# Two buffers in turn, in place of one allocated anew, for a norm's product of input and root

## The chip, the cores and the metric

One core of one Trainium2 chip runs the whole program in one launch. The metric is device time in microseconds (us) of that core, the median of the runs shown; lower is better. The names of the engines are those of the profile: PE is TensorE (PEld its weight loads), DVE is VectorE, ACT is ScalarE, POOL is GpSimd, SP is SyncE, which issues the DMAs.

## The reference, cut to what matters

Two layers of a block with four sequence mixers side by side, on 512 latent and 256 context tokens of width 1024. What the change touches is `modulate`, which stands ahead of the mixers and ahead of the feed-forward part in each layer.

```python
def rms_norm(x, g, eps=NORM_EPS):
    xf = x.astype(jnp.float32)
    y = xf * lax.rsqrt(jnp.mean(xf * xf, axis=-1, keepdims=True) + eps)
    return (y * g.astype(jnp.float32)).astype(x.dtype)

def modulate(x, g, shift, scale):
    return rms_norm(x, g) * (1 + scale) + shift
...
    for i in range(DEPTH):
        ...
        h_l = modulate(x, norm_mix_g[i], mod_l[0], mod_l[1])
        h_c = modulate(xc, norm_mix_g[i], mod_c[0], mod_c[1])
        pa_l, pb_l, pc_l, pd_l = _cumsplit(h_l @ w_in[i], MIXER_IN)
        ...
        x = x + mod_l[2] * (o_l @ w_out[i])
        x = x + mod_l[5] * conv_ffn(modulate(x, norm_ffn_g[i], mod_l[3], mod_l[4]),
                                    ffn_w_up[i], ffn_conv_w[i], ffn_conv_b[i], ffn_w_down[i])
```

## The kernel before

**Tiling.** The activations lie with their 1024 features on the partitions, as KD = 8 tiles `x[k]` of 128 features by up to 768 tokens. Each norm makes eight tiles `h[k]`, and each of these holds two halves, a high part `HL[:, 0]` and a low part `HL[:, 1]`, which the three matmuls of every product in `mm_feat` (L392) and the token-major products of `win_tok` (L770) read.

**The norm.** For each k, DVE multiplies `x[k]` by its scale and by the root into a scratch tile `y` (L641). ACT adds the shift and writes the high part (L643). For k = 0, 2, 3, 5 and 6 DVE makes the low part from `y` and the high part (L645). For k = 1, 4 and 7 (`k % 3 == 1`) ACT adds the shift into `y` in place (L648) and POOL makes the low part (L650). So `y` of k = 1, 4 and 7 is held until POOL is done with it.

There are seven such loops: the start norm of layer 0 (512 and 256 tokens one after the other under one `y` of 768 columns, the root `rs` in a tile of the on-chip memory SBUF), and then the feed-forward norm of layer 0, the mixer norm of layer 1 and the feed-forward norm of layer 1, each in two parts of tokens, a first loop and a second one (512 and 256 tokens, in the last norm 256 and 256). In these three the root lies in a bank of PSUM, the memory that PE writes (`pst`).

**Weights.** `weights` loads a piece by DMA, ACT writes its high part (L382, 512 or 288 columns) and POOL the low part (L383). POOL's queue is served in the order of the program, so these casts and the norm's L650 stand in one line. DVE's queue is in order too.

**Buffers.** `new` asks the `Arena` for columns: 30 slabs of 24 units (64 columns each), all columns of a slab of one type at a time. `find` takes, among the free places, the one that was given back longest ago, with a price for breaking into a slab that lies whole and idle. A place that is taken again waits for all earlier readers of it. In the start norm the arena has one place alone at that price, slab 9, so every `y` there is the same memory. In the feed-forward norm of layer 0 the eight `y` of the first loop lie in eight different places (in slabs 20, 13, 26, 20, 29, 24, 28 and 24). In the first loop of the mixer norm of layer 1 they alternate between slab 22 and slab 27 from k = 1 on. In the feed-forward norm of layer 1 they lie in eight places again.

**Order.** Program text is written by generators that are woven by a pace (`weave`); a scheduler then puts each engine's instructions in an order that follows which of them depend on which. The order is fixed when the program is built.

Of the kernel before, what the change touches and what calls it, by code (L numbers as in the profile page):

```python
# [223 lines left out]
class Net:  # L224
# [386 lines left out]
    def norm(self, li, which, x, sts, h, parts, first=None):  # L611

        nc = self.nc
        sh, sc = (0, 1) if which == "nmg" else (3, 4)
        gs = self.small([P, 8, 2], "gs")
        nco = self.conds(li, sc)

        def scales(k, m):
            nc.vector.scalar_tensor_tensor(out=gs[:, k:k + m, :nco], in0=self.mod[li][:, sc * 8 + k:sc * 8 + k + m, :nco], scalar=1.0,
                                           in1=self.par(li, which, k, m).unsqueeze(2).to_broadcast([P, m, nco]),  # L620
                                           op0=ALU.add, op1=ALU.mult)

        if first is None:
            scales(0, 8)
        n = parts[-1][-1][1]
        for i, (segs, st) in enumerate(zip(parts, sts)):
            a0, b0 = segs[0][0], segs[-1][1]
            w = b0 - a0
            if first is not None:
                rs = yield from self.root_first(first)  # L630
            else:
                rs = yield from self.root(st, segs)
            for k in range(KD):
                if first is not None:
                    scales(k, 1)
                if i == 0:
                    h.append(self.new([2, n], F32R))
                y, HL = self.new([w]), h[k]
                for a, b, s in segs:
                    yv, shift = y[:, a - a0:b - a0], self.modvec(li, sh, s, k)  # L640
                    nc.vector.scalar_tensor_tensor(out=yv, in0=x[k][:, a:b], scalar=gs[:, k, s:s + 1], in1=rs[:, a - a0:b - a0],  # L641
                                                   op0=ALU.mult, op1=ALU.mult)
                    nc.scalar.activation(out=HL[:, 0, a:b], in_=yv, func=AF.Identity, bias=shift)  # L643
                    if k % 3 != 1:
                        nc.vector.scalar_tensor_tensor(out=HL[:, 1, a:b], in0=yv, scalar=shift, in1=HL[:, 0, a:b].bitcast(F32),  # L645
                                                       op0=ALU.add, op1=ALU.subtract)
                    else:
                        nc.scalar.activation(out=yv, in_=yv, func=AF.Identity, bias=shift)  # L648
                if k % 3 == 1:
                    nc.gpsimd.tensor_tensor(out=HL[:, 1, a0:b0], in0=y, in1=HL[:, 0, a0:b0].bitcast(F32), op=ALU.subtract)  # L650
                self.free(y)
                if which == "nmg" and i + 1 == len(parts):
                    self.free(x[k])
                yield 1500 * w / T
            self.free(rs)


    def ffn(self, li, x, h, done, S):
# [1287 lines left out]
```

## Time and profile before

| | |
|---|---|
| median of 3 runs | 2377.65 us (2375.9 to 2383.59) |
| profiled execution, its own time | 2371.69 us |
| its span, first to last instruction | 2369.8 us |
| mean granted clock of PE in it | 0.954 |
| PE busy | 2194.0 us (93%) |
| DVE, POOL, ACT busy | 1327.0, 995.9, 934.2 us |

The profile is of one execution. Its own time stands 5.96 us below the median of the runs and 1.9 us above its span. Busy shares are means over stages; a busy PE need not be PE at its full rate, because the ends of matmuls are modelled.

### The profile page before, as it was taken

Reading aid. Unit: us, or ns where it says so; the run is one execution under the profiler, and the core shown is the slowest. Engines: PE = TensorE matmul, PEld = TensorE weight load, DVE = VectorE, ACT = ScalarE, POOL = GpSimd, SP = SyncE. Lnnn points to the kernel's source line nnn. Section 1 sums busy time; section 2 is a strip of 40 time slices with the busy share of each in tenths; the row PEclk is TensorE's granted clock in tenths of the full one; section 3 lists DMA queues with packets and bytes.
Section 4 is the critical chain, followed back from the end, with each engine's and each line's share of the span. In section 5 each row is a group of like instructions: output and inputs, shape, how many; then the busy total and the mean of one; then the engine's idle time right before and its main releaser. Section 6 shows DMA issues by size and latency. Waiting matters only on the chain. (4 is left out here: it accounts for less than half of the span.)

```text
span 2369.8 us, 40603 instructions
## 1 busy us (share of the span) xinstructions
PE 2194.0 (93%) x15656; PEld 1852.1 (78%) x15656; DVE 1327.0 (56%) x2900; ACT 934.2 (39%) x1730; POOL 995.9 (42%) x999
## 2 busy tenths in 40 slices
PE   7989996889989999999999989995899979999999
PEld 3877786768768788888888877785778868888888
DVE  3143567878864696765445643378877565332323
ACT  3333222555564422322223443332465544433333
POOL 1433437123422344434434634455443224555556
PEclk7999997889999999999999989997889989999999
DMA  8322354433234243343333521144233242333334
GB/s 324 116 72 82 102 150 108 105 89 93 58 123 143 82 137 116 109 142 106 116 107 107 172 65 55 59 126 132 69 98 87 77 138 72 102 94 99 98 98 134
DMA packets 241265, 258.51 MB, mean 109 GB/s; under 512 B 102896, under 2 KB 186160, under 8 KB 241072
## 3 DMA queue, kind: packets, MB, share of 16 engines
q1 hardware_dynamic: 241072, 255.92, 36.1%
q8 instruction: 123, 2.02, 0.4%
q14 instruction: 70, 0.57, 0.1%
HBM read 209.69 MB, written 37.77 MB: 104 GB/s over the span
## 5 line engine op out<-in xcount | busy, mean ns | idle before, releaser
L392 PE MATMUL pst<-slab,slab 128*128 128x512 f32 (+1 forms) x6552 | 1236.5, 350 | 14.4 <-POOL slab L650 5.8
L392 PEld LDWEIGHTS pst<-slab,slab 128*128 128x128 f32 x6552 | 1049.6, 190 | 195.8 <-issue 11.3
L383 POOL TENSOR_TENSOR slab<-slab,slab 128x512 fp32r<-128x512 f32 (+1 forms) x428 | 563.7, 1326 | 661.1 <-ACT slab L382 621.3
L382 ACT CAST slab<-slab 128x512 fp32r<-128x512 f32 (+1 forms) x428 | 258.7, 612 | 592.3 <-PE pst L392 418.6
L770 PE MATMUL pst<-slab,slab 128*128 128x256 f32 (+1 forms) x1872 | 254.1, 295 | 9.3 <-POOL slab L383 8.0
L770 PEld LDWEIGHTS pst<-slab,slab 128*128 128x128 f32 x1872 | 242.4, 199 | 20.4 <-POOL slab L383 9.5
L432 PE MATMUL pst<-cst,slab 128*128 128x128 f32 (+1 forms) x968 | 166.4, 305 | 69.1 <-DVE slab L937 21.7
L683 DVE SCALAR_TENSOR_TENSOR slab<-pst,pp,slab 128x511 f32<-128x511 f32 x66 | 41.6, 658 | 299.2 <-ACT slab L680 299.2
L432 PEld LDWEIGHTS pst<-cst,slab 128*128 128x128 f32 (+1 forms) x968 | 120.6, 153 | 96.6 <-DVE slab L937 24.3
L1620 PE MATMUL pst<-slab,slab 128*128 128x128 f32 (+4 forms) x1320 | 160.8, 283 | 7.3 <-DVE slab L1646 3.4
L1620 PEld LDWEIGHTS pst<-slab,slab 128*128 128x128 f32 (+3 forms) x1320 | 132.3, 179 | 29.6 <-issue 14.6
L714 DVE SCALAR_TENSOR_TENSOR slab<-pst,fgate,slab 128x512 f32<-128x512 f32 (+1 forms) x144 | 88.2, 628 | 104.9 <-PE pst L392 104.7
L1020 ACT ACTIVATE slab<-pst,mx 128x768 f32<-128x768 f32 (+1 forms) x120 | 97.7, 815 | 67.6 <-DVE mx L1018 64.3
L1018 DVE TENSOR_REDUCE mx<-pst 128x1 f32<-128x768 f32 (+1 forms) x120 | 100.2, 846 | 35.6 <-PE pst L1012 20.1
L695 POOL TENSOR_TENSOR slab<-slab,slab 128x768 fp32r<-128x768 f32 (+1 forms) x44 | 73.9, 1680 | 70.2 <-ACT slab L694 70.2
L551 DVE SCALAR_TENSOR_TENSOR slab<-slab,slab 128x512 bf16<-128x512 f32 x104 | 92.2, 886 | 5.1 <-DMA slab<-in_modw_dram 3.5
L1048 PE MATMUL pst<-slab,slab 128*64 128x128 f32 x832 | 67.0, 290 | 5.0 <-DVE slab L429 2.9
L1031 ACT ACTIVATE slab<-slab,r 128x768 f32<-128x768 f32 (+1 forms) x80 | 67.7, 852 | 10.0 <-DVE r L1030 9.3
L689 ACT ACTIVATE slab<-slab 128x768 f32<-128x768 f32 (+1 forms) x44 | 32.4, 737 | 85.7 <-DVE slab L685 85.6
L694 ACT CAST slab<-slab 128x768 fp32r<-128x768 f32 (+1 forms) x44 | 32.1, 729 | 85.0 <-DVE slab L691 84.9
L1012 PE MATMUL pst<-slab,slab 128*128 128x384 f32 (+1 forms) x144 | 48.8, 407 | 14.0 <-ACT slab L1020 6.4
L1048 PEld LDWEIGHTS pst<-slab,slab 128*64 128x64 f32 x832 | 46.9, 141 | 18.1 <-DVE slab L429 6.3
(320 smaller groups left out, 2626.6 us busy)
## 6 DMA issues: line engine op xcount, KB each, us to landing
slab<-in_wup_dram SPq DMA_DIRECT2D x88, 512.0 KB, 3.7
slab<-in_modw_dram SPq DMA_DIRECT2D x112, 256.0 KB, 3.0
slab<-in_wdn_dram SPq DMA_DIRECT2D x48, 512.0 KB, 3.5
slab<-in_win_dram SPq DMA_DIRECT2D x46, 512.0 KB, 3.9
slab<-in_modp_dram SPq DMA_DIRECT2D x40, 512.0 KB, 7.0
slab<-in_wout_dram SPq DMA_DIRECT2D x16, 512.0 KB, 3.7
slab<-in_xT_dram SPq DMA_DIRECT2D x16, 384.0 KB, 5.3
slab<-kb SPq DMA_DIRECT2D x24, 256.0 KB, 3.0
```

What stands on the lines that cost most here:

```text
L382: nc.scalar.copy(out=w[0], in_=st[:, k:k + q])
L383: nc.gpsimd.tensor_tensor(out=w[1], in0=st[:, k:k + q], in1=w[0].bitcast(F32), op=ALU.subtract)
L392: self.nc.tensor.matmul(ps[:, a:b], w[i][k][:, cols], x[j][k][:, a:b], start=(k == 0 and q == 0), stop=(k == nk - 1 and q == 2))
L432: self.nc.tensor.transpose(out, a.bitcast(F32) if a.dtype != F32 else a, self.c["ident"])
L551: self.tc.keep_in_program_order(nc.vector.scalar_tensor_tensor(out=junk, in0=w, scalar=1.0, in1=self.sc[s][e], op0=ALU.mult, op1=ALU.mult, ...
L695: nc.gpsimd.tensor_tensor(out=HL[:, 1, :n], in0=th[:, :n], in1=HL[:, 0, :n].bitcast(F32), op=ALU.subtract)
L714: nc.vector.scalar_tensor_tensor(out=x[m][:, a:b], in0=ps[:, a:b], scalar=gate[:, m, s:s + 1], in1=x[m][:, a:b], op0=ALU.mult, op1=ALU.add)
L770: self.nc.tensor.matmul(ps[:, :n], h[i][k][:, t * P:(t + 1) * P], w[j][k], start=(k == 0 and q == 0), stop=(k == KD - 1 and q == 2))
L1018: nc.vector.tensor_reduce(out=mx, in_=sv, axis=AX.XY, op=ALU.max, negate=True)
L1020: nc.scalar.activation(out=p[m][:, a:].rearrange("p (e c) -> p e c", e=2 - a // hb), in_=sv, func=AF.Exp, bias=mx, accum_out=lsum[:, m:m + 1])
L1048: nc.tensor.matmul(acc[64 * e:64 * e + 64, :P], vs[e][:, i + j], aT[:, 256 * j + P * e:256 * j + P * e + P], start=(first and j == 0), sto ...
L1620: mm = lambda o, a, b, pos: nc.tensor.matmul(o, a, b, start=True, stop=True, tile_position=pos)
```

## The change

The two buffers `ys` are taken before the loop over k, used in turn, and both are given back after the loop with the root.

```diff
@@ -630,12 +630,13 @@
                 rs = yield from self.root_first(first)
             else:
                 rs = yield from self.root(st, segs)
+            ys = [self.new([w]) for _ in range(2)]
             for k in range(KD):
                 if first is not None:
                     scales(k, 1)
                 if i == 0:
                     h.append(self.new([2, n], F32R))
-                y, HL = self.new([w]), h[k]
+                y, HL = ys[k % 2], h[k]
                 for a, b, s in segs:
                     yv, shift = y[:, a - a0:b - a0], self.modvec(li, sh, s, k)
...
                 if k % 3 == 1:
                     nc.gpsimd.tensor_tensor(out=HL[:, 1, a0:b0], in0=y, in1=HL[:, 0, a0:b0].bitcast(F32), op=ALU.subtract)
-                self.free(y)
                 if which == "nmg" and i + 1 == len(parts):
                     self.free(x[k])
                 yield 1500 * w / T
-            self.free(rs)
+            self.free(rs, *ys)
```

No instruction is added to the arithmetic or taken from it. What moves is memory: which place each `y` has, and with that the place of nearly every buffer that is taken later, and the order that the scheduler makes of it. The lines of `norm` behind the new one stand one line lower in the change: L641 is L642 there, L645 is L646, L650 is L651.

The first place is DVE's queue in the start norm, k = 1 to 3, before. The first name is what is written, and the digits behind slab9 count its tiles: slab9_13 is `y` (and the root, in other columns of the slab), slab4_8 to slab5_9 are `x`, slab12_27 and slab13_28 are `h[2]` and `h[3]`. In brackets stands the engine or DMA queue whose signal the instruction waits for.

```order
L641 SCALAR_TENSOR_TENSOR slab9_13_108<-slab4_8_103,gs_24_294,slab9_13_108 128x512 [waits DMAHW4_49,DVE_49]
L641 SCALAR_TENSOR_TENSOR slab9_13_108<-slab4_8_103,gs_24_294,slab9_13_108 128x256 [waits DVE_49]
L477 TENSOR_TENSOR mod0_77<-pst_69,pp_75 128x2x2 [waits PE_49,Activation_49]
L619 SCALAR_TENSOR_TENSOR gs_24_294<-mod0_77,pp_75 128x2 [waits DVE_49]
L641 SCALAR_TENSOR_TENSOR slab9_13_108<-slab5_9_104,gs_24_294,slab9_13_108 128x512 [waits DMAHW5_49,Pool_49]
L641 SCALAR_TENSOR_TENSOR slab9_13_108<-slab5_9_104,gs_24_294,slab9_13_108 128x256 [waits Activation_49]
L645 SCALAR_TENSOR_TENSOR slab12_27_336<-slab9_13_108,mod0_77,slab12_27_336 128x512 [waits Activation_49]
L645 SCALAR_TENSOR_TENSOR slab12_27_336<-slab9_13_108,mod0_77,slab12_27_336 128x256 [waits Activation_49]
L641 SCALAR_TENSOR_TENSOR slab9_13_108<-slab5_9_104,gs_24_294,slab9_13_108 128x512 [waits DMAHW6_49,DVE_49]
```

The same place in the change, from the second half of k = 1 to the first of k = 4:

```order
L642 SCALAR_TENSOR_TENSOR slab8_12_107<-slab4_8_103,gs_24_294,slab9_13_108 128x256
L477 TENSOR_TENSOR mod0_77<-pst_69,pp_75 128x2x2 [waits PE_49,Activation_49]
L642 SCALAR_TENSOR_TENSOR slab9_13_108<-slab5_9_104,gs_24_294,slab9_13_108 128x512 [waits DMAHW5_49,DVE_49]
L642 SCALAR_TENSOR_TENSOR slab9_13_108<-slab5_9_104,gs_24_294,slab9_13_108 128x256 [waits DVE_49]
L619 SCALAR_TENSOR_TENSOR gs_24_294<-mod0_77,pp_75 128x2
L619 SCALAR_TENSOR_TENSOR gs_24_294<-mod0_77,pp_75 128x2 [waits DVE_49]
L646 SCALAR_TENSOR_TENSOR slab12_27_336<-slab9_13_108,mod0_77,slab12_27_336 128x512 [waits Activation_49]
L646 SCALAR_TENSOR_TENSOR slab12_27_336<-slab9_13_108,mod0_77,slab12_27_336 128x256 [waits Activation_49]
L642 SCALAR_TENSOR_TENSOR slab8_12_107<-slab5_9_104,gs_24_294,slab9_13_108 128x512 [waits DMAHW6_49,Pool_49]
L642 SCALAR_TENSOR_TENSOR slab8_12_107<-slab5_9_104,gs_24_294,slab9_13_108 128x256
L642 SCALAR_TENSOR_TENSOR slab9_13_108<-slab6_10_105,gs_24_294,slab9_13_108 128x512 [waits DMAHW7_49,DVE_49]
```

The wait for POOL has moved from the product of k = 2 to that of k = 3, and two products and one low part stand between it and the one that POOL reads.

The second place is POOL's queue at the same time, from the low part of k = 1 on, before:

```order
L650 TENSOR_TENSOR slab11_26_327<-slab9_13_108,slab11_26_327 128x768 [waits Activation_49]
L650 TENSOR_TENSOR slab14_29_352<-slab9_13_108,slab14_29_352 128x768 [waits Activation_49]
L383 TENSOR_TENSOR slab3_4_99<-slab17_5_100,slab2_3_98 128x288 [waits DMAHW6_49,Activation_49]
L383 TENSOR_TENSOR slab3_4_99<-slab17_5_100,slab3_4_99 128x288 [waits Activation_49] x2
L383 TENSOR_TENSOR slab0_1_96<-slab18_6_101,slab0_1_96 128x288 [waits PE_49,DMAHW7_49,Activation_49,Pool_49]
L383 TENSOR_TENSOR slab0_1_96<-slab18_6_101,slab0_1_96 128x288 [waits PE_49,Activation_49,Pool_49]
L383 TENSOR_TENSOR slab1_2_97<-slab19_7_102,slab1_2_97 128x288 [waits DMAHW0_49,Activation_49,Pool_49]
L650 TENSOR_TENSOR slab8_32_377<-slab9_13_108,slab8_32_377 128x768 [waits Activation_49]
```

In the change the low part of k = 7 (slab28) stands behind one cast of the weights of `glav`, not six:

```order
L651 TENSOR_TENSOR slab11_26_327<-slab8_12_107,slab11_26_327 128x768 [waits Activation_49]
L651 TENSOR_TENSOR slab14_29_352<-slab9_13_108,slab14_29_352 128x768 [waits Activation_49]
L383 TENSOR_TENSOR slab3_4_99<-slab17_5_100,slab2_3_98 128x288 [waits DMAHW6_49,Activation_49]
L651 TENSOR_TENSOR slab28_32_377<-slab8_12_107,slab28_32_377 128x768 [waits Activation_49]
L383 TENSOR_TENSOR slab3_4_99<-slab17_5_100,slab3_4_99 128x288 [waits Activation_49] x2
```

The third place is DVE's queue in the feed-forward norm of layer 0, in the change. There slab27 holds both `y` of the first loop (512 columns), slab25 and slab10 the two of the second (256 columns); slab15, slab25 and slab4 are `x` as the second name.

```order
L642 SCALAR_TENSOR_TENSOR slab27_23_171<-slab15_108_3829,gs_327_7141,pst_69 128x512 [waits PE_49]
L642 SCALAR_TENSOR_TENSOR slab27_23_171<-slab15_108_3829,gs_327_7141,pst_69 128x512
L642 SCALAR_TENSOR_TENSOR slab25_21_169<-slab15_108_3829,gs_327_7141,pst_69 128x256 [waits PE_49]
L646 SCALAR_TENSOR_TENSOR slab16_213_5541<-slab27_23_171,mod0_77,slab16_213_5541 128x512 [waits Activation_49]
L642 SCALAR_TENSOR_TENSOR slab10_88_3483<-slab15_108_3829,gs_327_7141,pst_69 128x256
L642 SCALAR_TENSOR_TENSOR slab27_23_171<-slab25_21_169,gs_327_7141,pst_69 128x512 [waits DVE_49]
L646 SCALAR_TENSOR_TENSOR slab16_213_5541<-slab25_21_169,mod0_77,slab16_213_5541 128x256 [waits Activation_49]
L642 SCALAR_TENSOR_TENSOR slab27_23_171<-slab4_8_103,gs_327_7141,pst_69 128x512 [waits Pool_49]
```

Before, the first loop's products came one after the other with no wait for POOL, and the second loop's behind them; in the change the two loops are interleaved, and the product of k = 3 waits for POOL.

## Rows read from the trace of the kernel before

**Rows 1.** The page: PE's busy time, PE's busy tenths and its granted clock.

```profile
PE 2194.0 (93%) x15656; PEld 1852.1 (78%) x15656; DVE 1327.0 (56%) x2900; ACT 934.2 (39%) x1730; POOL 995.9 (42%) x999
...
PE   7989996889989999999999989995899979999999
...
PEclk7999997889999999999999989997889989999999
```

**Rows 2.** Busy time by stretch: from:to, length, engines with counts, clock, DMA.

```profile
41.50:76.40 34.90, 30.87 (x181) 21.79 (x177) 17.25 (x31) 17.36 (x37) 14.21 (x12) 0.96 0.46 157
...
830.00:1370.00 540.00, 536.76 (x3051) 466.96 (x3049) 328.50 (x604) 157.54 (x238) 237.20 (x159) 1.00 0.40 124
...
1600.00:1800.00 200.00, 157.69 (x1278) 135.46 (x1278) 163.53 (x414) 94.09 (x194) 85.79 (x145) 0.85 0.36 98
...
1641.80:1646.50 4.70, 4.27 (x19) 3.87 (x20) 4.26 (x19) 3.00 (x7) 0.00 (x0) 0.50 0.41 67
```

**Rows 3.** Waits of PE over the whole span: total us, times, longest.

```profile
PE pst L432 <- DVE slab L937: 21.7, 10, 7.1
...
PE pst L1465 <- DVE slab L1443: 10.1, 1, 10.1
```

**Rows 4.** DVE in order of time in the start norm: start, us, what.

```profile
48.39 1.15 DVE L641 SCALAR_TENSOR_TENSOR slab<-slab,gs,slab 128x512 f32<-128x512 f32 x2 [2.64 <-POOL slab L650]
49.93 1.15 DVE L645 SCALAR_TENSOR_TENSOR slab<-slab,mod,slab 128x512 fp32r<-128x512 f32 x2 [0.40 <-ACT slab L643]
...
58.12 0.16 DVE L477 TENSOR_TENSOR mod<-pst,pp 128x4 f32<-128x4 f32 x1 [3.12 <-PE pst L474]
58.43 2.23 DVE L641 SCALAR_TENSOR_TENSOR slab<-slab,gs,slab 128x512 f32<-128x512 f32 x2
60.58 2.23 DVE L645 SCALAR_TENSOR_TENSOR slab<-slab,mod,slab 128x512 fp32r<-128x512 f32 x2
```

**Rows 5.** POOL in order of time in the same stretch.

```profile
46.55 1.80 POOL L650 TENSOR_TENSOR slab<-slab,slab 128x768 fp32r<-128x768 f32 x1 [13.73 <-ACT slab L648]
...
58.36 2.96 POOL L383 TENSOR_TENSOR slab<-slab,slab 128x288 fp32r<-128x288 f32 x3
...
68.94 1.81 POOL L650 TENSOR_TENSOR slab<-slab,slab 128x768 fp32r<-128x768 f32 x1 [4.26 <-ACT slab L648]
71.98 0.80 POOL L383 TENSOR_TENSOR slab<-slab,slab 128x288 fp32r<-128x288 f32 x1 [1.23 <-ACT slab L382]
73.74 2.03 POOL L383 TENSOR_TENSOR slab<-slab,slab 128x288 fp32r<-128x288 f32 x2 [0.96 <-ACT slab L382]
```

**Rows 6.** ACT in order of time in the same stretch.

```profile
44.34 1.12 ACT L643 ACTIVATE slab<-slab,mod 128x512 fp32r<-128x512 f32 x2
45.36 1.11 ACT L648 ACTIVATE slab<-slab,mod 128x512 f32<-128x512 f32 x2
```

**Rows 7.** PE by line and shape, 41.5 to 76.4 us: count, busy us, mean ns, idle.

```profile
L392 PE MATMUL pst<-slab,slab 128*128 128x512 f32 x48 | 18.2, 437 | 3.4 <-POOL slab L650 2.6 <-ACT slab L643 0.8
...
L770 PE MATMUL pst<-slab,slab 128*128 128x288 f32 x29 | 5.6, 306 | 0.2 <-POOL slab L383 0.2
L470 PE MATMUL pst<-slab,slab 128*32 128x256 f32 x44 | 4.7, 457 | 0.0
L474 PE MATMUL pst<-cst,slab 128*128 128x2 f32 x12 | 1.6, 239 | 0.2 <-ACT slab L472 0.2
```

**Rows 8.** The same view of PE, 830 to 1370 us.

```profile
L392 PE MATMUL pst<-slab,slab 128*128 128x512 f32 x1515 | 517.2, 398 | 0.0
```

**Rows 9.** PE in order of time behind the start norm.

```profile
76.44 18.39 PE L770 MATMUL pst<-slab,slab 128*128 128x288 f32 x139
```

**Rows 10.** Waits of DVE, 1375 to 1400 us (mixer norm of layer 1).

```profile
DVE slab L641 <- POOL slab L650: 2.9, 2, 2.0
```

**Rows 11.** Waits of PE on POOL, 800 to 820 us, then 1375 to 1400 us.

```profile
PE pst L392 <- POOL slab L650: 0.8, 2, 0.6
...
PE pst L392 <- POOL slab L650: 1.9, 3, 1.1
```

## The prediction

> **What bounds the kernel now.** I began with the page. PE is busy for 2194.0 of 2369.8 us [rows 1], so most of the span is PE's work, and the change takes none of it away. What it can win or lose is time in which PE waits or runs slowly. The slices show where: the first ones, two groups in the middle of either layer (the mixers), and nothing in the feed-forward stages. The table by stretch says the same in microseconds: from 830 to 1370 us, the feed-forward of layer 0, PE lacks 3.2 of 540 us, from 1600 to 1800 us, the mixers of layer 1, 42.3 of 200 us at a mean granted clock of 0.85 [rows 2]. Then the list of PE's waits: in the mixers they are a handful of single long ones, such as 10.1 us on one DVE product at L1443 and 21.7 us in ten waits on L937 [rows 3]. Last I read the norms in order of time, engine by engine, since the change sits there.
>
> In the start norm the single `y` is a chain. DVE's product of k = 2 stands idle for 2.64 us until POOL's low part of k = 1 (46.55 us, 1.80 us long) has let go of `y` [rows 4, 5]. DVE's next long idle time, 3.12 us ahead of L477, ends in the product of k = 5 at 58.43 us [rows 4]. That product has to wait for POOL's low part of k = 4 in any case; L477, which waits for PE, only hides it. From 58.36 us on POOL casts weights, and DVE's pairs of halves take 2.23 us in place of 1.15 [rows 4, 5]. The last low part on POOL ends at 70.75, the last cast at 75.77, and at 76.44 PE begins a closed run of 139 products [rows 5, 9].
>
> **Does PE have room there?** From 41.5 to 76.4 us it runs 48 pairs of products of 512 and 256 columns, 29 of 288, 44 of L470 and 12 of L474 [rows 7]. A pair costs 536.76 / 1515 = 0.354 us where PE is saturated [rows 2, 8], a product of 288 columns 18.39 / 139 = 0.132 us [rows 9]. So 48 x 0.354 = 17.0, 29 x 0.132 = 3.8, and L470 and L474 at most the 4.7 and 1.6 us that they show: 27.1 of 34.9 us [rows 2]. At most 7.8 us can be won here, however fast DVE gets.
>
> **The change part by part.** *Start norm.* With two buffers the product of k = 2 no longer stands behind POOL. DVE is free at 48.39 - 2.64 = 45.75, so the product ends at 46.9. ACT is done with L648 at 46.47 [rows 6], writes the high part of k = 2 by 48.0, its first half by 47.6. The low part on DVE then meets POOL's L650, which runs to 48.35.
>
> Can the two run together? Beside POOL's casts the two halves of a product took 2.23 us in place of 1.15, so DVE lost 1.08 us, while POOL did 2.23 / 2.96 x 3 x 0.80 = 1.8 us of its own work [rows 4, 5]: DVE stood for some 60% of POOL's time. For a single long L650 I let it wait to the end, the worse case. The Trainium skill (SBUF — State Buffer, "Who interferes with whom") says that a DVE instruction with two inputs in SBUF and a GpSimd instruction that reads SBUF hold each other off, and whichever comes second waits for the whole instruction. By that rule the start comes out as below; by the 60% of the trace alone it would win 0.7 us more at each of two places.
>
> So the low part of k = 2 starts at 48.4 in place of 49.93, 1.5 us earlier. From there DVE has low part, product, low part, product with nothing to wait for (in the new order L477 stands behind the whole norm): 4 x 1.15 = 4.6, and the product of k = 5 starts at 53.0, not 58.43. The low part of k = 5 must let L650 of k = 4 pass (its `y` is ready 1.15 for the product, 0.5 for the last high half and 0.5 for the shift later, so at 54.0, and it ends at 55.8); then low part, product, low part, product of k = 5 to 7 take 4 x 1.15 = 4.6 us, to 60.5. Two more halves on ACT and the cast that stands between bring L650 of k = 7 to 61.8, where it started at 68.94 [rows 5]: 7.1 us earlier. It is faster than the waits alone because five casts now stand behind it, not ahead. They must be paid: seven casts of 0.80 us behind 63.6 end at 69.2, not 75.77, 6.6 us earlier. PE's closed run should begin 6 us earlier. I take **-6.0**. The low end is -1.5 (only the first wait goes, the rest is lost to casts and port), the high end -7.8. A loss of any weight I exclude here: every `y` is free no later than before, and at worst seven casts of 0.80 behind 70.75 would end at 76.35, 0.6 us late. PE is full behind 76.44, so what is won is not idle time that was there anyway.
>
> *Feed-forward norm of layer 0.* Here eight places become two a loop, and the change adds waits for POOL where there were none; behind the waiting product stand the low parts on which PE's products wait. The price is in the trace: the mixer norm of layer 1 alternated between two places already and lost 2.9 us of DVE to L650 [rows 10], and PE lost 1.9 us to POOL there against 0.8 in this norm [rows 11]. The difference at PE is 1.1. The new order interleaves the two loops and covers part of it. I take **+1.0**, ends 0 and +2.9.
>
> *Mixer norm of layer 1.* It has two places before and after; the second loop now comes in between and fills waits: **-0.5**, ends -2.9 (all of the wait goes) and +1.0. *Feed-forward norm of layer 1.* As in layer 0, with loops of half the length: **+0.5**, ends 0 and +1.5.
>
> *Everything else.* Nearly every later buffer has another place, so other reuses set other waits. In the feed-forward stages PE lacks 3 us in 540 [rows 2], nothing to win, and the other engines have slack to hide a wait. In the mixers it can go either way. One wait of the size of the longest single one is 10.1 us [rows 3]; I take **0** and the ends -10 and +12.5 (below).
>
> **Sum.** -6.0 + 1.0 - 0.5 + 0.5 = -5.0. The profiled execution took 2371.69 us and would take 2366.7. The median of the runs is 5.96 us above it, so the changed kernel's median should be 2377.65 - 5.0 = 2372.65, say **2372.7 us**. About 0.3% (7.1 us) is what a measurement of this kernel can tell from no change: under 2370.5 is faster, above 2384.8 slower.
>
> **Rivals.** *The start's gain is small.* If DVE and POOL block each other through the casts too, or PE's queue, which is in order, holds a product that waits for a late cast ahead of ready ones, only the first wait's 1.5 us is left, and the norms of the feed-forward take 1.5 back: 2377.7. For it: the casts are moved into a row behind L650, and POOL works them off alone. Against it: PE has 7.8 us of room and the last `h` comes 7 us earlier.
>
> *One long wait more in the mixers (slower).* At L1465 PE stood 10.1 us for DVE's product at L1443, and once only [rows 3]. DVE is busy there for 163.5 of 200 us [rows 2], so an operation that a reused place lets in late, or one that the new order puts ahead, makes PE wait in a second place. A wait of that size also lowers the granted clock: behind a wait of 7.1 us on L937 the profile shows 0.50 for another 4.7 us with 4.27 us of busy PE [rows 2, 3]; that work would take half as long at the upper level, so the wait costs about 2.4 us more. 10.1 + 2.4 = 12.5 on top of -5.0 gives 2385.2, slower. It decides from 12.1 us on (5.0 + 7.1); a second wait of only 7 us would leave no change. Against it: the order in the mixers follows the same dependences.
>
> *One long wait less in the mixers.* By the same reasoning the 10.1 us may go, by 8 to 10 us: 2363 to 2365. Nothing in the profile favours the one sign over the other.
>
> *The change does nothing.* Outside the start `y` mostly had several places already; were the start hidden, the time would be 2377 to 2379. PE's closed run from 76.44 speaks against it. I count it with the small gain.
>
> **How the numbers follow.** The start keeps its gain and the rest is even: 0.42, 2368 to 2378. Small or hidden gain: 0.17, 2375 to 2381. Longer waits in the mixers: 0.22, from 2383 up. Shorter ones: 0.19, below 2370. Of the first case I put 0.17 below 2370.5, since 2372.7 is only 2.2 us from that bound, and of the third 0.02 stays within. Faster: 0.19 + 0.17 = 0.36. Slower: 0.20. Same: 0.44. The range goes from 2361 to 2387: the low end is the sum with the longest mixer wait gone and 1.6 us more of the start, the high end the slower rival and 2 us. Beyond either end I leave about one chance in ten. The likeliest case's own range is 2368 to 2378.
>
> **What would show it.** In the changed profile the wait of L642 for L651 ahead of the product of k = 2 should be gone; the last L651 of the start should begin near 62, the last cast of `glav` near 69, PE's closed run of L770 near 70. In the feed-forward norm of layer 0 DVE should show one to three us of waits for L651, and PE's waits on it should go from 0.8 to about 1.9. The feed-forward stages should keep their length within 1 us. The prediction is wrong if PE's closed run starts later than 74, or if the stretches from there to the first feed-forward norm, or from 1420 to 1980, change by more than 5 us.

## The result, and the profile after

The changed kernel takes 2402.56 us (median of 4 runs, 2401.3 to 2404.56) against 2376.78 us of the kernel before beside it (4 runs, 2374.79 to 2383.59): a ratio of 1.0117, 95% interval 1.0094 to 1.014 (the quotient of the two medians is 1.0108, inside that interval). It is slower by 26 us. The profiled execution took 2404.56 us with a span of 2402.7 us, 32.9 us more than that of before. It is the slowest of its four runs, and the profiled execution of before was a fast one, so some 7 of the 32.9 us are the scatter of single executions. In the lines from 634 to 651 the numbers stand one higher than before (L641 is L642, L650 is L651).

The page of the change first, PE's busy time, its busy tenths and its granted clock, as in [rows 1]:

```profile
PE 2212.3 (92%) x15656; PEld 1860.7 (77%) x15656; DVE 1340.4 (56%) x2900; ACT 936.1 (39%) x1730; POOL 1004.9 (42%) x999
...
PE   7989996799989899999999989985799989999999
...
PEclk8999997889899999999999999997789999999999
```

Same 15656 products, 18.3 us more of PE's busy time, and the thin slices are again those in the mixers. To place the loss I matched the traces: the n-th product of each line and shape before with the n-th after; the edge of a stage moves by the median shift of the products within 8 us of it. By that the start is 4.8 us faster (0.4 was lost on entry already), the mixers of layer 0 take 14.4 us more, the feed-forward norm of layer 0 2.4 more, the mixer norm of layer 1 1.6 less, the mixers of layer 1 19.0 more and the last norm 3.5 more. With 0.3 us less between norm and mixers of layer 1 this makes 0.4 - 4.8 + 14.4 + 2.4 - 1.6 - 0.3 + 19.0 + 3.5 = 33.0, the 32.9 of the span. The feed-forward stages keep their length within 0.1 us.

The start is what was asked for. In the change, DVE and then POOL in order of time, to be held against [rows 4, 5]:

```profile
45.67 0.16 DVE L477 TENSOR_TENSOR mod<-pst,pp 128x4 f32<-128x4 f32 x1 [2.42 <-PE pst L474]
45.78 2.71 DVE L642 SCALAR_TENSOR_TENSOR slab<-slab,gs,slab 128x512 f32<-128x512 f32 x2
48.56 1.14 DVE L646 SCALAR_TENSOR_TENSOR slab<-slab,mod,slab 128x512 fp32r<-128x512 f32 x2
...
54.60 2.21 DVE L646 SCALAR_TENSOR_TENSOR slab<-slab,mod,slab 128x512 fp32r<-128x512 f32 x2 [0.29 <-ACT slab L644]
```

```profile
45.93 2.28 POOL L651 TENSOR_TENSOR slab<-slab,slab 128x768 fp32r<-128x768 f32 x1 [13.09 <-ACT slab L649]
54.04 1.83 POOL L651 TENSOR_TENSOR slab<-slab,slab 128x768 fp32r<-128x768 f32 x1 [5.83 <-ACT slab L649]
...
61.38 1.84 POOL L651 TENSOR_TENSOR slab<-slab,slab 128x768 fp32r<-128x768 f32 x1 [0.73 <-ACT slab L649]
63.18 5.39 POOL L383 TENSOR_TENSOR slab<-slab,slab 128x288 fp32r<-128x288 f32 x7
```

No product waits for POOL's L651 any more; the last L651 starts at 61.38, not 68.94, and seven casts end at 68.57. PE behind it:

```profile
66.58 3.34 PE L770 MATMUL pst<-slab,slab 128*128 128x288 f32 x24
69.84 1.07 PE L470 MATMUL pst<-slab,slab 128*32 128x256 f32 x16
70.84 0.79 PE L770 MATMUL pst<-slab,slab 128*128 128x288 f32 x4
71.47 0.54 PE L474 MATMUL pst<-cst,slab 128*128 128x2 f32 x4
71.87 18.39 PE L770 MATMUL pst<-slab,slab 128*128 128x288 f32 x139
```

The closed run begins at 71.87, not 76.44 [rows 9], and PE no longer waits for the casts: what stands ahead follows without a gap. So the loss lies in the two mixer stages, none of whose statements the change touches. Their windows, first of before, then of the change (length, then busy time with counts, last clock, DMA share, GB/s):

```profile
78.00:784.00 706.00, 639.26 (x5463) 535.89 (x5462) 421.51 (x1028) 296.87 (x599) 252.14 (x319) 0.93 0.36 102
...
1556.00:1982.00 426.00, 363.91 (x3287) 311.48 (x3286) 300.55 (x722) 203.86 (x413) 166.94 (x235) 0.92 0.39 105
```

```profile
73.60:794.00 720.40, 648.34 (x5462) 541.73 (x5461) 419.87 (x1030) 296.95 (x600) 258.55 (x319) 0.92 0.35 100
...
1566.40:2011.40 445.00, 374.47 (x3287) 315.13 (x3286) 311.58 (x720) 204.61 (x413) 167.67 (x235) 0.91 0.37 101
```

Length less PE's busy time is PE's idle time: 66.7 and 72.1 us in layer 0, 62.1 and 70.5 in layer 1. So of the 14.4 us 5.3 are idle, of the 19.0 us 8.4; the rest, 9.1 and 10.6 us, is the same products taking longer. Part of that is the clock: by the trace's clock record PE was at the lower of its two levels for 119.5 us of the mixers of layer 0 (95.6 before) and for 78.5 us of those of layer 1 (71.7 before). Half of each difference, 12 and 3.4 us, is an estimate of the most that this costs. It covers the longer products of layer 0 and only a third of those of layer 1.

### The profile page after: what moved, and what is told of

The parts are those of the page before. It is cut to its first block, busy times and chain, and to the rows that moved or that the text cites. A ratio compares the mean times of both kernels' runs of the same rounds, so it can differ in the third digit from the quotient of the medians.

```text
span 2402.7 us, 40609 instructions
## 1 busy us (share of the span) xinstructions
PE 2212.3 (92%) x15656; PEld 1860.7 (77%) x15656; DVE 1340.4 (56%) x2900; ACT 936.1 (39%) x1730; POOL 1004.9 (42%) x999
## 5 line engine op out<-in xcount | busy, mean ns | idle before, releaser
L770 PE MATMUL pst<-slab,slab 128*128 128x256 f32 (+1 forms) x1872 | 256.1, 297 | 29.2 <-POOL slab L383 13.3
L770 PEld LDWEIGHTS pst<-slab,slab 128*128 128x128 f32 x1872 | 244.6, 200 | 39.4 <-POOL slab L383 14.0
L432 PE MATMUL pst<-cst,slab 128*128 128x128 f32 (+1 forms) x968 | 171.1, 305 | 60.9 <-DVE slab L937 24.0
L432 PEld LDWEIGHTS pst<-cst,slab 128*128 128x128 f32 (+1 forms) x968 | 119.6, 152 | 91.3 <-DVE slab L937 24.3
L1620 PE MATMUL pst<-slab,slab 128*128 128x128 f32 (+5 forms) x1304 | 157.9, 280 | 9.4 <-DVE slab L1646 3.2
L1020 ACT ACTIVATE slab<-pst,mx 128x768 f32<-128x768 f32 (+1 forms) x120 | 97.7, 816 | 73.3 <-DVE mx L1018 72.2
L551 DVE SCALAR_TENSOR_TENSOR slab<-slab,slab 128x512 bf16<-128x512 f32 x132 | 113.8, 862 | 4.9 <-DMA slab<-in_modw_dram 2.9
L695 POOL TENSOR_TENSOR slab<-slab,slab 128x768 fp32r<-128x768 f32 (+1 forms) x44 | 74.1, 1685 | 72.2 <-ACT slab L694 72.2
L1048 PE MATMUL pst<-slab,slab 128*64 128x128 f32 x808 | 69.2, 299 | 7.1 <-DVE slab L429 5.2
L1707 POOL TENSOR_TENSOR slab<-cst,pcu 64x256 f32<-64x256 f32 x48 | 30.9, 644 | 83.1 <-PE pst L1620 41.1
```

The source lines that it names most:

```text
L432: self.nc.tensor.transpose(out, a.bitcast(F32) if a.dtype != F32 else a, self.c["ident"])
L551: self.tc.keep_in_program_order(nc.vector.scalar_tensor_tensor(out=junk, in0=w, scalar=1.0, in1=self.sc[s][e], op0=ALU.mult, op1=ALU.mult, ...
L695: nc.gpsimd.tensor_tensor(out=HL[:, 1, :n], in0=th[:, :n], in1=HL[:, 0, :n].bitcast(F32), op=ALU.subtract)
L770: self.nc.tensor.matmul(ps[:, :n], h[i][k][:, t * P:(t + 1) * P], w[j][k], start=(k == 0 and q == 0), stop=(k == KD - 1 and q == 2))
L1020: nc.scalar.activation(out=p[m][:, a:].rearrange("p (e c) -> p e c", e=2 - a // hb), in_=sv, func=AF.Exp, bias=mx, accum_out=lsum[:, m:m + 1])
L1048: nc.tensor.matmul(acc[64 * e:64 * e + 64, :P], vs[e][:, i + j], aT[:, 256 * j + P * e:256 * j + P * e + P], start=(first and j == 0), sto ...
```

## The experiments

Two theories. **Places**: the second buffer does in the norms what it should; what costs is that both are held through the loop, so that nearly every later buffer gets another place, with it other waits and another order of each queue. **Two buffers**: the alternation itself lets engines run ahead and makes something later stand. The first four kernels take the change apart.

*a_two_old_places.* The start norm alone, with the allocator's books as before:

```diff
+            if first is not None:
+                odd = self.slabs.tile([P, Arena.SLAB * Arena.GRAN], F32, tag="slab29", name="odd", bufs=1)[:, :w]
...
+                own = y
+                if first is not None and k % 2:
+                    y = odd
...
-                self.free(y)
+                self.free(own)
```

> The kernel before, but the start norm's product alternates between its own slab and one that lies unused until the mixers; the allocator's books and every place handed out later are those of before, and so is each engine's order from the start's end on. Later norms keep what they had. Theory 'places' (the two buffers gain in the start, the loss comes from where all later buffers land and from the order that follows): the closed run of token-major matmuls starts 4 to 5 us earlier than in the kernel before, mixers of both layers keep their lengths within 2 us, total 2371 to 2374 (4 to 6 below before). Rival 'two buffers' (the alternation itself makes something later stand): the mixers grow as in the change, total 2390 or more.

2370.66 us, ratio 0.9989 (0.9978 to 1.0). The start gains 4.5 us, the mixers are 707.0 and 426.6 us long, 1.0 and 0.6 more than in before. By time it lies 2.1 us below the kernel before beside it, where 4 to 6 were expected.

*d_one_new_places.* The places of the change, one buffer used:

```diff
-                y, HL = ys[k % 2], h[k]
+                y, HL = ys[0], h[k]
```

> The change with one index: every norm holds its two buffers as in the change, but uses the first of them for all eight products, so the places of all buffers are those of the change and the use of one buffer is that of before. Theory 'places': the mixers of layer 0 still take some 18 us more than in before, those of layer 1 some 19 more; the start's gain of 4.5 is gone and the later norms lose a little from one buffer alone: 2404 to 2415. Rival 'two buffers': with one buffer in use the loss of 25 is gone, 2376 to 2385.

2412.55 us, ratio 1.0161 (1.0139 to 1.0184). The start's gain is gone, the mixers of layer 1 lose 23.6 us. This falls to "places". Its mixers of layer 0, however, lose only 2.6 us where 18 were expected: their idle time is that of the change (72.2 us), their busy time is not (636.4 against 648.3). The last section comes back to it.

*s_start_only* and *l_later_only.* The change in the first norm or in the later three alone, the other norms as before:

```diff
+            two = first is not None
+            ys = [self.new([w]) for _ in range(2)] if two else []
...
+                y, HL = ys[k % 2] if two else self.new([w]), h[k]
...
+                if not two:
+                    self.free(y)
```

(`first is None` in the other.)

> The change in the first norm alone; the three later norms take and free one buffer a product as in before. Up to the first FFN norm each engine's order and every place is that of the change, afterwards the places are a new draw, neither those of before nor of the change. Theory 'places': start 4.5 less and mixers of layer 0 some 18 more, exactly as in the change (first FFN norm about 10 later than before); mixers of layer 1 are a new draw, anywhere from 10 less to 20 more than in before: total 2377 to 2407. Rival 'two buffers in the later norms' is what costs: mixers of layer 0 would be as in before and the total 2372.

2391.1 us, ratio 1.0072 (1.0053 to 1.0092). Mixers of layer 0 11.4 us longer, of layer 1 14.9. The expectation's 18 for layer 0 had counted from the best point behind the start; from edge to edge the change had 14.4.

> The change in the three later norms alone; the first norm as before. Up to the first FFN norm each engine's order and every place is that of before, afterwards the places are a new draw. Theory 'places': start and mixers of layer 0 equal before within 1 us; the two FFN norms with two halves of one slab cost 2 to 4 us each as in the change, since before's places for the product were already several; mixers of layer 1 a new draw, from 10 less to 20 more: total 2372 to 2403. Rival 'two buffers in the first norm make the mixers of layer 0 late' is not excluded by this run, but one that puts the loss on the later norms' two buffers expects 2400 or more here.

2387.68 us, ratio 1.0059 (1.0039 to 1.0079). Start and mixers of layer 0 as before (706.1 us), the two feed-forward norms 3.5 us longer each, the mixers of layer 1 8.6 longer: a new draw in the range named.

*after_again.* The change a second time, for its profile.

> The change once more, unedited, for a second profile of it. In the first profile the mixers of layer 0 lost 14.5 us against before, some 5 of them as idle time of TensorE and 9 as a lower granted clock; the kernel with one buffer in use, whose queues there stand in the same order and whose waits are the same, lost 2.6. If the clock's part is luck of one execution, this profile shows the mixers of layer 0 within 5 us of before; if it repeats with the order and its timing, 11 to 15 again, and the lower clock at the same gaps near 618 to 636. Mixers of layer 1: 19 again by either. Time 2401 to 2405.

2400.06 us, one execution. Layer 0's mixers lose 9.5 us this time, layer 1's 18.3. The first value lies under the 11 to 15 of a repeat and over the 5 of luck: about half repeats.

*u_hold, u_turn4, u_away28.* No norm is changed. Each edit gives later buffers other places:

```diff
         self.weave(start())
+        hold = self.new([256])
```

```diff
-    LOW, TURN, BREAK, AWAY = 17, 5, 100, 30
+    LOW, TURN, BREAK, AWAY = 17, 4, 100, 30
```

(and 28 for AWAY in the third).

> The kernel before, with no norm changed: after the first norm it reserves 256 columns of buffer that nothing ever writes or reads, so that the allocator hands out other places for what follows. Same instructions, same work. Theory 'places': start and first norm equal before within 1 us, the mixers of either layer a new draw, each from 5 less to 20 more; total 2372 to 2410, and a difference of more than 3 us from before in at least one mixer stage. Rival 'the loss belongs to the norms' two buffers': within 3 us of before in each stage, total within 0.3%.

> The kernel before with no norm changed and one number of the allocator's pricing moved from 5 to 4, which moves later buffers to other places from the middle of layer 0's mixers on. Theory 'places': everything up to some 300 us equal before; then each mixer stage a new draw, from 5 less to 20 more; total 2372 to 2410. Rival 'two buffers': within 0.3% of before.

> The kernel before with no norm changed and another number of the allocator's pricing moved from 30 to 28, a third draw of places for all that follows the first 250 us or so. Theory 'places': each mixer stage a new draw, from 5 less to 20 more; total 2372 to 2410. Rival 'two buffers': within 0.3% of before. If this and the other two redraws all come out slower than before, the places of before are a good draw rather than a middling one, and a change that redraws them pays for that on average.

2395.42 us, ratio 1.0083 (1.0054 to 1.0112); 2382.71, 1.0051 (1.003 to 1.0072); 2386.5, 1.0047 (1.0019 to 1.0074). All slower, by the mixers of layer 1: 18.2, 10.0 and 11.0 us more. A buffer that nothing touches costs two thirds of what the change costs.

*f_load_place.* One wait of the changed order by itself. In the change SP's queue in layer 1's mixers, in order of time:

```profile
1618.37 1.57 SPq L1509 DMA_DIRECT2D slab<-scrin  x2
...
1628.86 1.25 SPq L1509 DMA_DIRECT2D slab<-scrin  x2
1630.15 0.61 SPq L1626 DMA_DIRECT2D slab<-vt  x1
1630.81 1.06 SPq L376 DMA_DIRECT2D slab<-in_win_dram  x2
```

The list of SP's waits from 1605 to 1650 us says what the second L1509 waited for (total us, times, longest):

```profile
SPq L1509 <- DVE slab L1438: 8.1, 1, 8.1
```

A load of the recurrent scan stands ahead of two weight loads and waits for its place. PE, in order of time, then stands twice for those weights:

```profile
1635.29 0.80 PE L770 MATMUL pst<-slab,slab 128*128 128x256 f32 x2 [8.12 <-ACT slab L382]
1645.06 1.22 PE L770 MATMUL pst<-slab,slab 128*128 128x256 f32 x4 [8.97 <-POOL slab L383]
```

The edit was meant to put that one buffer into a slab that is idle:

```diff
             nd, ao = BD[d][i % 2], self.new([4, 64])
+            if (li, d, i) == (1, 0, 0):
+                at = self.shaped(self.slab[24][:, 0:256], [4, 64])
+                self.held[id(at)] = (at,) + self.held.pop(id(ao))[1:]
+                ao = at
```

> The change with one 256-column buffer of layer 1's recurrent scan (the first chunk's block of scores, loaded at L1509) put into a slab that is idle instead of the place that the allocator gives it, and nothing else: all other places stay, and the engines' queues keep their order but for 4 entries on SP, 4 on POOL, 2 on ACT, 5 on VectorE and some 26 matmuls. In the change that load stands on SP's queue ahead of two weight loads and waits 8.1 us for VectorE; the weights then come late and TensorE stands 8.1 us for their cast and 9.0 us for their split. Theory 'places act through the order of the queues': without that wait the weight load leaves some 10 us earlier (near 1621 in place of 1630.8), the two waits of TensorE shrink from 17 together to under 11, and layer 1's mixers give back 4 to 10 us: 2392 to 2399. Rival 'the weights' split was late anyway', since POOL is held by the features' chain until 1643: the load leaves earlier, TensorE stands as long for POOL, and the total stays at 2400 to 2405.

2395.91 us, ratio 1.0104 (1.0084 to 1.0124), within the change's interval. The first weight load leaves at 1613.33 in this run, where the stage is 8.4 us ahead of the change's, so 9 us earlier. The second stays behind the scan's load, which still waits for DVE, and longer than in the change. The list of SP's waits from 1600 to 1645 us (the load's L1509 is L1513 in this kernel):

```profile
SPq L1513 <- DVE slab L1442: 10.6, 1, 10.6
```

So slab 24 was not idle: in this program L1442 of DVE still reads the columns that the load is to overwrite. The edit did not take the wait away, it let one of the two weight loads out from behind it. PE:

```profile
1620.95 0.38 PE L770 MATMUL pst<-slab,slab 128*128 128x256 f32 x1 [2.14 <-ACT slab L382]
1631.29 3.13 PE L770 MATMUL pst<-slab,slab 128*128 128x256 f32 x13 [9.96 <-POOL slab L383]
...
1638.68 3.83 PE L770 MATMUL pst<-slab,slab 128*128 128x256 f32 x15 [4.04 <-POOL slab L383]
```

17.1 us of waits have become 16.1: the cast comes 6 us sooner to PE, and PE stands for POOL, whose next piece of that weight is queued behind L1446, which waits for DVE. The mixers of layer 1 take 447.8 us, nothing is given back there; where this profile is shorter than that of the change it is in layer 0's mixers (710.6 us), which the edit does not reach. The total lies in the range of the theory and below that of the rival, but not by the stage that the theory named. What is shown is this much: with the first weights on their way 9 us earlier PE's products with POOL's part of them begin 5.4 us earlier in the stage (1631.29 in place of 1645.06), then PE stands 4.0 us for POOL's part of the second weights, and nothing of it is left. That speaks for the rival, POOL being held by other work. What the scan's wait costs stays open, because no run here is without it.

*c_all_two_old.* The counterpart to d: the change's two buffers in all four norms, with every other place and, outside the norms, every queue's order as before. To the edit of a comes

```diff
+            else:
+                q, s0 = {(0, "nfg", 0): (24, 0), (0, "nfg", 1): (24, 16), (1, "nmg", 0): (26, 0), (1, "nmg", 1): (26, 0),
+                         (1, "nfg", 0): (23, 0), (1, "nfg", 1): (23, 0)}[li, which, i]
+                two = [self.slab[q][:, s0 * 64 + e * w:s0 * 64 + e * w + w] for e in range(2)]
...
+                if first is None:
+                    y = two[k % 2]
+                elif k % 2:
+                    y = odd
```

> The change's two buffers in turn in all four norms, with the place of every other buffer and every queue's order outside the norms as in the kernel before: the allocator keeps the books of before, and each later norm's products alternate between two halves of a slab that is idle during it. Theory 'places': start 4 to 4.5 less; the two FFN norms 2 to 4 us longer each, since before gave their eight products eight places and two in turn are fewer; mixer norm of layer 1 from 2 less to 1 more; layer 0's mixers 705 to 710 and layer 1's 424 to 428 as in before (706 and 426), not 716 to 721 and 444 to 448 as in the change. Total within 5 us of before, ratio 0.998 to 1.002. Rival 'two buffers': the mixers lengthen as in the change, 2390 or more.

2372.98 us, ratio 1.0002 (0.9986 to 1.0018). Its windows from the start's end to the last norm:

```profile
73.70:780.40 706.70, 639.26 (x5462) 535.74 (x5462) 422.19 (x1034) 297.69 (x601) 253.09 (x319) 0.93 0.35 104
780.40:821.30 40.90, 34.81 (x199) 29.37 (x198) 28.12 (x73) 20.38 (x37) 16.41 (x14) 0.83 0.24 78
...
1556.30:1983.30 427.00, 364.66 (x3287) 311.92 (x3286) 300.60 (x722) 203.61 (x413) 167.49 (x235) 0.91 0.38 105
1983.30:2034.80 51.50, 46.79 (x292) 40.70 (x291) 28.93 (x70) 25.40 (x49) 24.73 (x22) 0.97 0.21 66
```

Two buffers without the new places cost nothing and win nothing: the mixers are those of before to 1 us, the feed-forward norms are longer by 2.9 and 3.5 us, and that eats the start.

*a_again.* The one version that might beat the kernel before, in five rounds.

> The version with the second buffer in the start norm alone and all other places as before, timed in five rounds to see whether it beats the kernel before by more than the measurement can miss. From the first profile of it (start 4.1 less, layer 0's mixers 1.0 more, layer 1's 0.6 more): 2.5 to 4.5 less, ratio 0.998 to 0.9995. Rival 'two buffers cost elsewhere': ratio 1.000 or more.

2371.17 us, ratio 0.9998 (0.9986 to 1.001). The start gains 4.0 us in its profile once more, but by time it is not told from before. No version here beats the kernel before by more than can be measured.

All stages side by side, in us, from one profile each; "start" is the shift behind the start norm less that at 20 us, in brackets PE's idle time, the length less PE's busy time:

| kernel | start | mixers 0 | ff norm 0 | mixers 1 | ff norm 1 |
|---|---|---|---|---|---|
| before | 0 | 706.0 (66.7) | 38.0 | 426.0 (62.1) | 48.0 |
| the change | -4.8 | 720.4 (72.1) | 40.4 | 445.0 (70.5) | 51.5 |
| after_again | -4.8 | 715.5 (73.3) | 40.2 | 444.3 (68.5) | 52.0 |
| f_load_place | -4.1 | 710.6 (72.3) | 40.3 | 447.8 (66.3) | 51.9 |
| d_one_new_places | -0.3 | 708.6 (72.2) | 40.0 | 449.6 (69.9) | 52.1 |
| s_start_only | -4.4 | 717.4 (71.6) | 38.6 | 440.9 (71.6) | 48.4 |
| l_later_only | -0.3 | 706.1 (67.6) | 41.5 | 434.6 (68.4) | 51.5 |
| u_hold | -0.3 | 704.7 (76.2) | 39.3 | 444.2 (75.7) | 47.9 |
| u_turn4 | -0.3 | 705.2 (71.1) | 37.7 | 436.0 (70.1) | 48.0 |
| u_away28 | -0.1 | 703.4 (69.9) | 39.0 | 437.0 (68.9) | 49.3 |
| a_two_old_places | -4.5 | 707.0 (66.9) | 38.0 | 426.6 (62.5) | 48.0 |
| a_again | -4.0 | 708.4 (68.2) | 38.6 | 424.8 (61.9) | 49.1 |
| c_all_two_old | -4.7 | 706.7 (67.4) | 40.9 | 427.0 (62.3) | 51.5 |

## Why the prediction was wrong

**The step that failed is "everything else", 0 with ends -10 and +12.5.** It measured +33.4 in the two mixer stages together (+27.8 in the second profile of the change), and each of them moved by more than the 5 us that the prediction had named as a sign of being wrong. Three things in it were wrong. It took the new places as one event, while there are two stages of over 400 us, each drawn anew. It took the size from the longest single wait, and misread that too: besides the 10.1 us at L1465, PE's list of before has a longer wait in the mixers of layer 1, at L432 (total us, times, longest):

```profile
PE pst L432 <- DMA slab<-od: 12.9, 1, 12.9
...
PE pst L770 <- POOL slab L383: 5.0, 3, 3.0
```

Both long waits are gone in the change (L1465 waits 1.0 us for that product), and yet the stage is 19.0 us longer. PE now stands for weights at L770:

```profile
PE pst L770 <- POOL slab L383: 13.3, 3, 9.0
PE pst L770 <- ACT slab L382: 10.3, 2, 8.1
```

So the loss is a sum over many waits (idle time +5.3 and +8.4 us) and over products and DVE instructions that run longer, not one wait more or less. And it found that "nothing in the profile favours the one sign": the profile of one kernel cannot say so, since it shows one draw. The runs do. With the places of before the mixers of layer 1 took 424.8 to 427.0 us in four profiles; in six other sets of places (of the change and of s, l and the three u) they took 434.6 to 449.6. None was better. In layer 0 the draw of before is a middling one: the three u took 703.4 to 705.2.

**The slower rival** had the sign and the stage, not the mechanism. The 10.1 us wait at L1465 went, as the opposite rival had hoped, and did not help: PE stood for weights instead (8.1 and 9.0 us), and in f, where the first of them leave earlier, it stood 10.0 us for POOL. The rival's price for the clock was read from the wrong wait. The clock stood at 0.50 through the whole 7.1 us on L937, so it had fallen before it:

```profile
1634.80:1641.80 7.00, 0.00 (x0) 0.00 (x0) 5.42 (x28) 0.41 (x1) 3.85 (x10) 0.50 0.22 60
```

The wait of 10.1 us does show a fall: 1.00 from 1610.8 to 1614.4 us, while PE stood, and 0.50 from 1614.5 to 1624.6. What the new order does to DVE can be seen at L1447, four instructions of the same size, before and after (duration min/median/max in ns):

```profile
L1447 DVE TENSOR_TENSOR slab<-slab,slab x4: 678/678/684, 1560.5 to 1621.8; 128x512 f32<-128x512 f32 x4
```

```profile
L1447 DVE TENSOR_TENSOR slab<-slab,slab x4: 676/1230/2289, 1571.8 to 1636.1; 128x512 f32<-128x512 f32 x4
```

The traces show what stands beside the two long ones. In the change a POOL instruction had started just before each of them, and DVE's ended 0.54 us behind POOL's (1609.40 and 1608.86, 1638.42 and 1637.88 us). The second of them, POOL and then DVE:

```profile
1635.97 1.91 POOL L1446 TENSOR_TENSOR slab<-slab,slab 128x768 f32<-128x768 f32 x1 [0.50 <-DVE slab L1445]
```

```profile
1636.13 2.29 DVE L1447 TENSOR_TENSOR slab<-slab,slab 128x512 f32<-128x512 f32 x1
```

That is the picture that the start norm shows (below): the new order lets POOL's instruction begin first, and DVE stands behind it. It is no rule without exception: in before the last of the four also began behind a POOL instruction, L855, and took its 0.68 us, while POOL's took 2.12. In all, DVE's busy time in this stage goes from 300.6 to 311.6 us for the same work. That all 11 us come about so is not shown, nor how much of them reaches PE. Which part of the new order carries most of the 8.4 us of idle time stays open, and no run here parts a place's own waits from the order that the scheduler makes of the places.

**Start norm, -6.0: measured -4.8 to -4.0.** Mechanism right, size off. The chain of DVE and POOL came out as worked out: the low part of k = 2 at 48.56 (48.4 forecast), the last L651 at 61.38 (61.8), the last of the seven casts done at 68.57 (69.2). The closed run came at 71.87, not near 70, because PE had become the bound. "At most 7.8 us can be won" priced PE's work ahead of it at 27.1 us; the window from 41.5 to 72.0 shows 28.80 us busy in 30.5, 1.7 us more than priced. The stand of DVE behind POOL that the prediction took as the worse case is there: the product of k = 2 took 2.71 us in place of 1.14 and ended at 48.49, behind POOL's 48.21. This row agrees with the rule of the Trainium skill that the prediction cites (SBUF — State Buffer, "Who interferes with whom").

**Feed-forward norms, +1.0 and +0.5: measured +2.4 and +3.5**, in c +2.9 and +3.5, in l +3.5 each, and next to nothing where the norm takes a buffer anew for each product (s: 0.6 and 0.4). The reason was right, eight places become two. The size was off, most in layer 1, where I had halved it because its loops are shorter. Of the signs named for layer 0 one came, PE's waits on POOL, 1.8 us from 794 to 834 us in place of 0.8 (about 1.9 forecast); the one to three us of DVE's waits for L651 did not, the list of that stage has none. In layer 1 PE's waits on POOL show the chain, in the change 2.5 us, in before 0.5:

```profile
PE pst L392 <- POOL slab L651: 2.5, 2, 1.3
```

```profile
PE pst L392 <- POOL slab L650: 0.5, 1, 0.5
```

DVE's own waits for L651 are short there (0.5 us in all), yet the last L651 starts 18.8 us behind the root's first L604 (2047.21 less 2028.39) where L650 needed 14.8 (2013.77 less 1998.97). **Mixer norm of layer 1, -0.5: measured -1.6**, and from -1.8 to +1.2 in other runs with two buffers; not to be told from nothing. With one buffer held (d) it lost 3.7.

So the norms' own terms sum to -4.8 + 2.4 - 1.6 + 3.5 = -0.5 us, not -5.0. c agrees: its interval, 0.9986 to 1.0018 or -3.3 to +4.3 us, holds -0.5 and not -5.0.

## What to carry to other kernels

Where an allocator picks places by when they were given back, and a scheduler orders queues by those places, holding a buffer longer is an edit of the whole program behind it: ask first whether the edit can be made with every other place kept (a buffer outside the allocator's books), then the local gain can be measured at all. Hold a buffer that nothing uses, or move one number of the allocator, before you believe in a local cause: three such kernels, with no norm changed, lost 0.5 to 0.8%. And count what the code gives in fact, not what it says: "one buffer" was eight places in the feed-forward norms, and two in turn were fewer.

## What the hardware showed that I had not expected

The change and d have the same order of products here and reach this place within 0.03 us of each other. PE waits 1.9 us for the same ACT instruction in both. First the change, PE in order of time and the window around it:

```profile
618.92 0.60 PE L1778 MATMUL pst<-lora,slab 128*128 128x256 f32 x2
621.41 0.50 PE L1012 MATMUL pst<-slab,slab 128*128 128x256 f32 x2 [1.90 <-ACT slab L1020]
...
622.04 2.80 PE L1620 MATMUL pst<-slab,slab 128*128 128x128 f32 x10
```

```profile
618.00:640.00 22.00, 19.60 (x113) 14.95 (x114) 11.99 (x46) 7.39 (x24) 8.97 (x17) 0.61 0.14 35
```

Then d, the same two views:

```profile
618.95 0.60 PE L1778 MATMUL pst<-lora,slab 128*128 128x256 f32 x2
621.43 0.50 PE L1012 MATMUL pst<-slab,slab 128*128 128x256 f32 x2 [1.89 <-ACT slab L1020]
...
622.06 1.57 PE L1620 MATMUL pst<-slab,slab 128*128 128x128 f32 x10
```

```profile
618.00:640.00 22.00, 18.63 (x168) 14.79 (x168) 17.41 (x58) 10.22 (x29) 8.13 (x17) 0.92 0.16 41
```

Behind the same short wait the same ten products take 2.80 us in one execution and 1.57 in the other. In the change the clock falls to its lower level, 1.2 GHz, right behind that wait and stays there (0.50 from 622.0 to 639.0 us). In d it is still at the upper level (1.00 from 619.6 to 629.9), falls behind a later wait of 1.0 us, at 630.0, and is up again from 633.5 us on. The mean granted clock from 618 to 640 us is 0.61 in the change and in s, 0.73 in after_again, 0.92 in f and d. In the five profiles in which layer 0's mixers run in the changed order PE's idle time lies between 71.6 and 73.3 us, and the stage takes 708.6 to 720.4. The length follows the time at the lower level, by the clock record 88.7 us in d, 95.6 in f, 105.8 in after_again, 116.1 in s and 119.5 in the change. The change, after_again and f run one and the same program up to there and still differ by 9.8 us. So of layer 0's 14.4 us only the 5.3 of idle time can be put down to the order; of the rest the runs with the changed order show anything between -2.8 (d) and +9.1.
